# VectorE's 512-column mask, group norm and output operations of a scan as two halves of 256

## The chip, the cores and the metric

The kernel runs on one core of a Trainium2 chip. The metric is the device time of one execution in microseconds (us), the median of several runs. All times below are us unless marked ns. The engines are named as the profile names them: PE (TensorE, matrix products), DVE (VectorE), ACT (ScalarE), POOL (GpSimd) and SP (SyncE, whose queue starts most of the DMAs).

## The reference

The program is a decoder trunk of two layers on an input of 512 tokens by 2048 channels in float32. Layer 0 has a projection, attention, pooling and gates and is not touched. Layer 1 is an RWKV-7 time mixing with 32 heads of 64 channels. Six mixes of the input are projected to r, k, v, g, a decay w and a rate a; then a state of 64 x 64 per head runs over the tokens, and its output goes through a group norm, a bonus and a gate into the output projection:

```python
def step(state, inp):
    r_t, w_t, k_t, v_t, kk_t, a_t = inp
    sa = jnp.einsum('bhvk,bhk->bhv', state, -kk_t)
    state = (state * w_t[:, :, None, :]
             + sa[..., None] * (kk_t * a_t)[:, :, None, :]
             + v_t[..., None] * k_t[:, :, None, :])
    return state, jnp.einsum('bhvk,bhk->bhv', state, r_t)
...
o = wkv7_scan(r, decay, k, v, kk, a)
mean = jnp.mean(o, axis=-1, keepdims=True)
var = jnp.mean(jnp.square(o - mean), axis=-1, keepdims=True)
o = ((o - mean) * lax.rsqrt(var + GN_EPS)).reshape(B_, S, D) * gn_w + gn_b
bonus = jnp.sum(r * k * r_k, axis=-1, keepdims=True) * v
o = (o + bonus.reshape(B_, S, D)) * jax.nn.silu(g)
return o.astype(x.dtype) @ w_o
```

## The kernel before

Layer 0 and the projections k, r and g of layer 1 are large products in which every float32 operand is split into two parts and three products are summed (lines 137 to 147 and 506 to 508). The work around the change is the scan, `scan()`, which treats the 32 heads as 16 pairs of two heads, and the 512 tokens as 8 chunks of 64. A tile of one pair has 128 partitions (two heads of 64 channels, or 64 tokens of a chunk by two) and 512 or 1024 columns.

For each pair p there are seven generators; each `yield` ends a step:

- `vproj(p)` projects v for the pair: 48 products of 512 columns on PE (lines 145 to 147, tile vps), with the weights split by ACT (L137) and by POOL (L141, tile wlo).
- `gprod(p)` loads AR and BK, multiplies them chunk by chunk (L908, tile g in PSUM, two tiles of four chunks for each half b), and puts a triangular mask on them: L914 writes Z[h] from g[h] and mk, one operation of 512 columns for each half b and head h, four for a pair. Then BK is transposed (L920) and copied by ACT (L921).
- `lanes(p)` inverts the 16 x 16 diagonal blocks: POOL copies blocks of Z to nd (L950, four operations; two of them read Z[0], two Z[1]), DVE transposes (L955, tile lt) and adds (L957, tile la), then come 15 times a product (L962, tile pr) and a reduction (L963, tile uc) of growing size, each of which reads what the one before it wrote; ACT spreads the result (L969, tile e), DVE transposes (L971, tile tb), ACT writes DT (L973), DVE transposes it into U (L977). The tile uc is the same for all pairs.
- `levels(p)` extends the inverse to 64 x 64 with PE, ACT and DVE (L1000 to L1026).
- `vprep(p)` makes the bonus bv on POOL (L930), and the transposed v (L937, L940).
- `chain(p)` is the recurrence over the 8 chunks: PE's xo (L1044, L1047), copied to xs by DVE (L1051) and ACT (L1052); PE's sa (L1055), copied into RS by DVE (L1056); PE's s (L1062); DVE's new state M (L1071 or L1073) from s and ACT's m (L1066); PE's output (L1076), copied to O by ACT (L1079).
- `post(p)` is the group norm and the output of the pair: a sum over each head's 64 columns (L1091, tile gs), the subtraction of the mean in O (L1093), ACT's square (L1095), its sum (L1097), a reciprocal root in small operations (L209 to L220), the multiplication (L1100), four transposes on PE (L1104, tile ot), ACT's scale and shift (L1106, tile gm), the bonus and the gate (L1108, L1109), and a store or a split. Its DVE operations have 512 columns.

The scan is cut into periods of 12 slots, one pair each; in a slot, the chain of one pair and that of the next are advanced under a high priority (an offset of 400), and the steps of the other generators follow at planned times, given by constants such as LA = (8, 15) for the lanes of pair p + 3, GP = (0.5, 9) for its gprod and PO = (13.5, 20) for the post of pair p. PE's order is that of the program, by hand. On the other engines the framework sets the order: an instruction that is ready goes by its priority, which is its place in the program, or 400 places earlier for the chains.

Pools have few buffers: one uc, one nd2, one gs, two of the PSUM tiles g, bt, vt and ot together, three O, four Z of each head.

Of the kernel before, what the change touches and what calls it, by code (L numbers as in the profile page):

```python
# [12 lines left out]
ALU = mybir.AluOpType  # L13
AX = mybir.AxisListType
# [3 lines left out]
P = 128  # L18
# [16 lines left out]
class Kernel:  # L35
# [809 lines left out]
    def scan(self, ctx, xv, first, mp, ld, ar_d, bk_d, bc_d, g_d, m_d):  # L845
        nc, tc, i = self.nc, self.tc, self.i
# [47 lines left out]
        def gprod(p):  # L894

            s = sets[p]
            AR = s["AR"] = ld.tile([P, 8, 2, 64], F32, tag="AR", name="AR", bufs=4)
            nc.sync.dma_start(AR.rearrange("p a b c -> p (a b c)"), ar_d[p])
            BK = ld.tile([P, 8, P], F32, tag="BK", name="BK")
            nc.sync.dma_start(BK.rearrange("p a b -> p (a b)"), bk_d[p])  # L900
            yield

            Z = s["Z"] = [st.tile([P, 8, P], F32, tag=f"Z{h}", name=f"Z{h}", bufs=4) for h in range(2)]
            for b in range(2):
                g = [aux("g").rearrange("p (c n) -> p c n", c=4) for _ in range(2)]
                for c in range(4):
                    for h in range(2):
                        mm(g[h][:, c, :], BK[half[h], 4 * b + c, :],  # L908
                           AR[half[h], 4 * b + c].rearrange("p a b -> p (a b)"), start=True, stop=True)
                    if c == 1:  # L910
                        yield
                for h in range(2):
                    mk = self.mk[:, 64 * (p % 2):64 * (p % 2) + P]
                    nc.vector.tensor_mul(Z[h][:, 4 * b:4 * b + 4, :], g[h], mk.unsqueeze(1).to_broadcast([P, 4, P]))  # L914
                yield
            BT = s["BT"] = st.tile([P, 8, P], F32, tag="BT", name="BT")
            for b in range(2):
                g = aux("bt")
                for c in range(4):
                    nc.tensor.transpose(g[:, c * P:(c + 1) * P], BK[:, 4 * b + c, :], self.ident)  # L920
                nc.scalar.copy(BT[:, 4 * b:4 * b + 4, :], g.rearrange("p (c n) -> p c n", c=4))  # L921
                yield
# [160 lines left out]
        def post(p):  # L1083

            s = sets[p]
            gt = tp.tile([P, S], F32, tag="ldg", name="ldg")
            nc.sync.dma_start(gt, g_d[p])
            O = s["O"].rearrange("p t h n -> p (t h) n")
            sm = tp.tile([P, 8], F32, tag="gs", name="gs")
            bc = lambda t: t.unsqueeze(2).to_broadcast([P, 8, 64])  # L1090
            nc.vector.tensor_reduce(sm, O, AX.X, ALU.add)  # L1091
            yield
            nc.vector.scalar_tensor_tensor(O, bc(sm), -1.0 / 64, O, ALU.mult, ALU.add)  # L1093
            sq = tp.tile([P, 8, 64], F32, tag="pt", name="gsq")
            nc.scalar.activation(sq, O, AF.Square)  # L1095
            yield
            nc.vector.tensor_reduce(sm, sq, AX.X, ALU.add)  # L1097
            rs = self.rsqrt_eps(tp, sm, GN_EPS, 8, "gn", 1.0 / 64)
            yield
            nc.vector.tensor_mul(O, O, bc(rs))  # L1100
            yield
            g = aux("ot")
            for t in range(4):
                nc.tensor.transpose(g[:, t * P:(t + 1) * P], s["O"][:, t].rearrange("p h n -> p (h n)"), self.ident)  # L1104
            m = tp.tile([P, S], F32, tag="pt", name="gm")
            nc.scalar.activation(m, g, AF.Identity, scale=self.vec["gw"][:, p:p + 1], bias=self.vec["gb"][:, p:p + 1])  # L1106
            yield
            nc.vector.tensor_add(m, m, s["bv"])  # L1108
            nc.vector.scalar_tensor_tensor(m, m, 0.5, gt, ALU.mult, ALU.mult)  # L1109
            if p < 13:  # L1110
                nc.sync.dma_start(m_d[p], m)
            else:
                t = mixed[p] = mp.tile([P, 2, S], F32R, tag="mx", name="mixed")
                self.split(t[:, 0, :], t[:, 1, :], m)
            yield
# [67 lines left out]
        def plan_pair(base, q, skip=0):  # L1183

            gp = gprod(q)
            next(gp)
            plan(base, gp, 6, *GP)
            plan(base, hurry(lanes(q)) if q == 15 else lanes(q), 18, *LA)
            plan(base, hurry(levels(q)) if q == 15 else levels(q), 5, *LV)
            plan(base, vproj(q), 8, *VJ)  # L1190
            plan(base, vprep(q), 2, *VP)


        v, gp = vproj(0), gprod(0)
        next(gp)
        for q in range(2):
# [6 lines left out]
        for q in range(16):  # L1203
            next(la)
            if q % 2:
                next(v, None)
        g1, v = gprod(1), vproj(1)
        next(g1)
        run(la)
# [18 lines left out]
        for p in range(-1, 16):  # L1228
            at = 12 * (p + 1)
            if p + 3 < 16:  # L1230
                plan_pair(at, p + 3)
            if 0 <= p < 15:
                late = 1.2 if p in (13, 14) else 0
                plan(at, post(p), 6, PO[0] + late, PO[1] + late)
            if p == 13:
                plan(at, units(0, 1, 2), 3, *A13)
                plan(at, project(*both(0, 1, 2)), 6, *B13)
            if p == 14:
                plan(at, units(3, 4, 5, 6, 7), 5, *A14)
                plan(at, project(*both(3, 4, 5, 6, 7)), 10, *B14)  # L1240
                plan(at, project(*[(2, k) for k in range(3)]), 3, *Q14)
            if p == 15:
                plan(at, units(8, 9, 10, 11, 12, 13), 6, *A15)
                plan(at, project(*both(8, 9, 10, 11, 12, 13)), 12, *B15)
                plan(at, project(*[(2, k) for k in range(3, 10)]), 7, *Q15)
            B = chain(p + 1) if p < 15 else None
            slot(at, [c for c in (A, B) if c])
            A = B
        assert not todo
        g = post(15)  # L1250
        for _ in range(4):
            next(g)
# [87 lines left out]
```

## Time and profile before

| | us |
|---|---|
| median of 3 runs (lowest to highest) | 2084.72 (2082.19 to 2085.89) |
| the profiled execution | 2082.21 |
| its span, first to last instruction | 2080.4 |
| granted PE clock in it | 0.992 |
| 1390 to 1490, start of the scan: DVE busy | 77.69 of 100 |
| 1490 to 1580: DVE busy, PE busy | 78.90, 87.71 of 90 |
| 1580 to 1640: DVE busy, PE busy | 52.26, 57.44 of 60 |
| 1820 to 1880, end of the scan with the first output products: DVE, PE busy | 48.82, 52.98 of 60 |

The profile is that of one execution. An engine's busy time counts its computing instructions; matrix products are pipelined with modelled ends, so a busy PE is not PE at its peak. Rows of instructions name the line, the engine, the operation and the tiles as out<-in, with partitions x columns. A chain of waits follows the work that ended last back in time: at each step to what released it, or to the instruction before it on its engine. An instruction on DVE may start before the one ahead of it on DVE has ended, so the time from start to start can be less than a duration.

### The profile page before, as it was taken

Reading aid. Unit: us, or ns where it says so; the run is one execution under the profiler, and the core shown is the slowest. Engines: PE = TensorE matmul, PEld = TensorE weight load, DVE = VectorE, ACT = ScalarE, POOL = GpSimd, SP = SyncE. Lnnn points to the kernel's source line nnn. Section 1 sums busy time; section 2 is a strip of 40 time slices with the busy share of each in tenths; the row PEclk is TensorE's granted clock in tenths of the full one; section 3 lists DMA queues with packets and bytes.
Section 4 is the critical chain, followed back from the end, with each engine's and each line's share of the span. In section 5 each row is a group of like instructions: output and inputs, shape, how many; then the busy total and the mean of one; then the engine's idle time right before and its main releaser. Section 6 shows DMA issues by size and latency. Waiting matters only on the chain.

```text
span 2080.4 us, 33934 instructions
## 1 busy us (share of the span) xinstructions
PE 2016.8 (97%) x13091; PEld 1637.4 (79%) x13091; DVE 1282.0 (62%) x2572; ACT 961.5 (46%) x1687; POOL 282.7 (14%) x550
## 2 busy tenths in 40 slices
PE   8999999999999998999999999999999999989996
PEld 7888888888888897777878888886777777767786
DVE  5344345444433357666866676668788888886436
ACT  3345445323322138654745564454555555564221
POOL 0000000000000000234000000013444444410003
PEclk9999999999999999999999999999999999999998
DMA  5222222233333353465365556542223332232733
GB/s 195 92 81 81 81 81 66 86 97 100 98 111 112 115 169 126 138 180 178 118 213 190 181 171 218 198 166 67 91 76 106 109 108 89 95 118 92 245 105 111
DMA packets 214034, 262.99 MB, mean 126 GB/s; under 512 B 15769, under 2 KB 161777, under 8 KB 213105
## 3 DMA queue, kind: packets, MB, share of 16 engines
q1 hardware_dynamic: 213872, 260.83, 38.6%
q8 instruction: 103, 1.69, 0.3%
q14 instruction: 59, 0.48, 0.1%
HBM read 214.32 MB, written 46.47 MB: 125 GB/s over the span
## 4 chain that ended last, share of the span: by engine, by line
PE 77%; DVE 14%; ACT 3%; issue 2%; DMA 2%; POOL 1%; SPq 0%; DVEq 0%; ACTq 0%; POOLq 0%
PE ga L145 16%; PE ga L146 16%; PE ga L147 16%; PE gb L506 4%; PE gb L508 4%; PE gb L507 4%; DVE pr L962 2%; PE vps L145 2%; DVE uc L963 1%; DVE M L1071 1%; PE vps L146 1%; PE vps L147 1%; DVE RS L1056 1%; PE g L908 1%; PE y L506 1%
## 5 line engine op out<-in xcount | busy, mean ns | idle before, releaser
L141 DVE TENSOR_TENSOR wlo<-wraw,whi 128x1024 fp32r<-128x1024 f32 (+1 forms) x268 | 314.1, 1175 | 467.3 <-ACT whi L137 464.0
L137 ACT CAST whi<-wraw 128x1024 fp32r<-128x1024 f32 (+1 forms) x324 | 303.0, 938 | 545.2 <-PE ga L146 297.9
L145 PE MATMUL ga<-mx,whi 128*128 128x512 f32 x768 | 299.9, 391 | 3.2 <-ACT mx L137 3.2
L146 PE MATMUL ga<-mx,whi 128*128 128x512 f32 x768 | 300.4, 391 | 1.6 <-DVE mx L141 1.6
L145 PE MATMUL ga<-x,whi 128*128 128x512 f32 x768 | 300.5, 391 | 0.1
L147 PE MATMUL ga<-mx,wlo 128*128 128x512 f32 x768 | 300.3, 391 | 0.0
L147 PE MATMUL ga<-x,wlo 128*128 128x512 f32 x768 | 299.5, 390 | 0.5 <-DVE wlo L141 0.5
L146 PE MATMUL ga<-x,whi 128*128 128x512 f32 x768 | 299.2, 390 | 0.0
L508 PE MATMUL gb<-wlo,mixed 128*128 128x512 f32 (+1 forms) x576 | 197.4, 344 | 2.8 <-DVE wlo L141 2.8
L506 PE MATMUL gb<-whi,mixed 128*128 128x512 f32 (+1 forms) x576 | 198.0, 344 | 1.6 <-DVE s L457 1.6
L507 PE MATMUL gb<-whi,mixed 128*128 128x512 f32 (+1 forms) x576 | 197.5, 343 | 0.0
L145 PEld LDWEIGHTS ga<-mx,whi 128*128 128x128 f32 x768 | 144.8, 189 | 36.3 <-ACT mx L137 3.6
L146 PEld LDWEIGHTS ga<-mx,whi 128*128 128x128 f32 x768 | 144.9, 189 | 32.9 <-DVE mx L141 1.9
L147 PEld LDWEIGHTS ga<-mx,wlo 128*128 128x128 f32 x768 | 144.8, 189 | 30.6
L147 PEld LDWEIGHTS ga<-x,wlo 128*128 128x128 f32 x768 | 144.2, 188 | 31.2 <-DVE wlo L141 1.0
L145 PEld LDWEIGHTS ga<-x,whi 128*128 128x128 f32 x768 | 144.2, 188 | 29.6 <-ACT whi L137 0.4
L146 PEld LDWEIGHTS ga<-x,whi 128*128 128x128 f32 x768 | 144.3, 188 | 29.1
L141 POOL TENSOR_TENSOR wlo<-wraw,whi 128x128 fp32r<-128x128 f32 x224 | 100.3, 478 | 221.9 <-ACT whi L137 195.1
L508 PEld LDWEIGHTS gb<-wlo,mixed 128*128 128x128 f32 x576 | 109.4, 190 | 16.4 <-DVE wlo L141 3.7
L506 PEld LDWEIGHTS gb<-whi,mixed 128*128 128x128 f32 x576 | 109.5, 190 | 16.0 <-DVE s L457 3.3
L507 PEld LDWEIGHTS gb<-whi,mixed 128*128 128x128 f32 x576 | 109.6, 190 | 12.5
L145 PE MATMUL vps<-mx,whi 128*128 128x512 f32 x256 | 113.4, 443 | 0.8 <-ACT vT L891 0.8
(333 smaller groups left out, 3347.7 us busy)
## 6 DMA issues: line engine op xcount, KB each, us to landing
wraw<-in_ev_w_in SPq DMA_DIRECT2D x96, 512.0 KB, 3.6
wraw<-in_ev_w_out SPq DMA_DIRECT2D x32, 512.0 KB, 3.6
wraw<-in_od_w_k SPq DMA_DIRECT2D x32, 512.0 KB, 4.7
wraw<-in_od_w_r SPq DMA_DIRECT2D x32, 512.0 KB, 3.4
wraw<-in_od_w_g SPq DMA_DIRECT2D x32, 512.0 KB, 3.8
wraw<-in_od_w_v SPq DMA_DIRECT2D x64, 256.0 KB, 2.8
ar_d<-pAR SPq DMA_DIRECT2D x16, 512.0 KB, 2.6
bk_d<-pBK SPq DMA_DIRECT2D x16, 512.0 KB, 3.2
```

The lines of the kernel that those rows point to most:

```text
L137: self.nc.scalar.copy(hi, src)
L141: (eng or self.nc.vector).tensor_sub(lo[:, sl], src[:, sl], hi[:, sl].bitcast(F32))
L145: mm(ps, ah, bh, start=start, stop=False)
L146: mm(ps, ah, bl, start=False, stop=False)
L147: mm(ps, al, bh, start=False, stop=stop)
L506: mm(ps, ah, bh, start=start, stop=False)
L507: mm(ps, al, bh, start=False, stop=False)
L508: mm(ps, ah, bl, start=False, stop=stop)
L908: mm(g[h][:, c, :], BK[half[h], 4 * b + c, :], AR[half[h], 4 * b + c].rearrange("p a b -> p (a b)"), start=True, stop=True)
L962: nc.vector.tensor_mul(q, uc[:, :t, :t], la[:, t, :t].unsqueeze(1).to_broadcast([P, t, t]))
L963: nc.vector.tensor_reduce(uc[:, :t, t], q, AX.X, ALU.add)
L1056: nc.vector.tensor_copy(RS[a, c], sa[a])
```

## The change

In `scan()` the ten DVE operations of 512 columns in a pair's masks and post are issued as two operations of 256 columns each, with the same values:

```diff
@@ gprod
-                    nc.vector.tensor_mul(Z[h][:, 4 * b:4 * b + 4, :], g[h], mk.unsqueeze(1).to_broadcast([P, 4, P]))
+                    for c in (0, 2):
+                        nc.vector.tensor_mul(Z[h][:, 4 * b + c:4 * b + c + 2, :], g[h][:, c:c + 2], mk.unsqueeze(1).to_broadcast([P, 2, P]))
@@ post
-            bc = lambda t: t.unsqueeze(2).to_broadcast([P, 8, 64])
-            nc.vector.tensor_reduce(sm, O, AX.X, ALU.add)
-            yield
-            nc.vector.scalar_tensor_tensor(O, bc(sm), -1.0 / 64, O, ALU.mult, ALU.add)
+            for a in (0, 4):
+                nc.vector.tensor_reduce(sm[:, a:a + 4], O[:, a:a + 4], AX.X, ALU.add)
+            yield
+            bc = lambda t: t.unsqueeze(2).to_broadcast([P, 4, 64])
+            for a in (0, 4):
+                nc.vector.scalar_tensor_tensor(O[:, a:a + 4], bc(sm[:, a:a + 4]), -1.0 / 64, O[:, a:a + 4], ALU.mult, ALU.add)
             sq = tp.tile([P, 8, 64], F32, tag="pt", name="gsq")
             nc.scalar.activation(sq, O, AF.Square)
             yield
-            nc.vector.tensor_reduce(sm, sq, AX.X, ALU.add)
+            for a in (0, 4):
+                nc.vector.tensor_reduce(sm[:, a:a + 4], sq[:, a:a + 4], AX.X, ALU.add)
             rs = self.rsqrt_eps(tp, sm, GN_EPS, 8, "gn", 1.0 / 64)
             yield
-            nc.vector.tensor_mul(O, O, bc(rs))
+            for a in (0, 4):
+                nc.vector.tensor_mul(O[:, a:a + 4], O[:, a:a + 4], bc(rs[:, a:a + 4]))
...
-            nc.vector.tensor_add(m, m, s["bv"])
-            nc.vector.scalar_tensor_tensor(m, m, 0.5, gt, ALU.mult, ALU.mult)
+            for a in (slice(0, 256), slice(256, 512)):
+                nc.vector.tensor_add(m[:, a], m[:, a], s["bv"][:, a])
+                nc.vector.scalar_tensor_tensor(m[:, a], m[:, a], 0.5, gt[:, a], ALU.mult, ALU.mult)
```

The number of yields and their places, and everything on PE, ACT, POOL and the DMA queues, are as before.

## The prediction

> **What bounds the kernel now.** I read the page first, then a table of engine time by stage, then the chain of waits and the waits inside the scan, and last the single instructions of one period of the scan. Times are us unless marked ns. In a timeline row the columns are start, duration, engine, line, operation, output and input with their shapes, count, and in brackets the idle time before it with what ended that.
>
> From the page, the span, the busy time of each engine and the chain by engine:
>
> ```profile
> span 2080.4 us, 33934 instructions
> PE 2016.8 (97%) x13091; PEld 1637.4 (79%) x13091; DVE 1282.0 (62%) x2572; ACT 961.5 (46%) x1687; POOL 282.7 (14%) x550
> PE 77%; DVE 14%; ACT 3%; issue 2%; DMA 2%; POOL 1%; SPq 0%; DVEq 0%; ACTq 0%; POOLq 0%
> ```
>
> Over the whole span TensorE is the bound. The change lies in the scan alone, so its worth is read there. One row of the table by stage (busy us and instruction count per engine), then the chain of waits for the same 60 us by line, then what waited for whom from 1580 to 1820 (us, times, longest):
>
> ```profile
> 1640.00:1700.00 60.00, 57.85 (x736) 43.50 (x735) 52.28 (x170) 35.17 (x92) 26.82 (x53) 1.00 0.31 98
> by line: DVE pr L962 11.0%; DVE M L1071 9.3%; DVE uc L963 8.7%; issue 8.4%; DVE Z L914 6.8%; DVE RS L1056 6.3%; POOL nd L950 4.9%; DVE xs L1051 4.5%; DVE U L1013 2.6%; ACT DT L973 2.5%; DVE U L1026 2.5%; PE vps L145 2.2%; DVE gm L1108 2.1%;
> DVE lt L955 <- POOL nd L950: 13.1, 8, 1.6
> PE s L1062 <- DVE RS L1056: 6.8, 17, 0.7
> ```
>
> The reader is to see three things. VectorE is busy 52.28 of 60 us (87%) and nearly every line of the chain is its own; TensorE is busy too (57.85), but what it waits for is VectorE's RS. And VectorE's one long wait is for POOL's nd, 13.1 us in 8 periods, 1.6 each. So in the scan there is a loop: the lanes' inversion (pr and uc, 30 operations, each of which needs the one before it) runs on VectorE, then ScalarE and VectorE turn it, then the next pair's masks, POOL's nd, the transpose lt, and the next inversion. Here is one round of that loop on VectorE, first its start, then its late part and its end:
>
> ```profile
> 1644.71 0.71 DVE L955 STREAM_TRANSPOSE lt<-nd 128x512 f32<-128x512 f32 x1 [1.63 <-POOL nd L950]
> ...
> 1645.81 0.69 DVE L1108 TENSOR_TENSOR gm<-gm,bv 128x512 f32<-128x512 f32 x1
> 1646.42 0.42 DVE L957 TENSOR_TENSOR la<-lt 128x256 f32<-128x256 f32 x1
> 1646.75 0.69 DVE L1109 SCALAR_TENSOR_TENSOR gm<-gm,ldg 128x512 f32<-128x512 f32 x1
> 1647.47 0.61 DVE L1056 COPY RS<-sa 64x128 f32<-64x128 f32 x2
> ...
> 1656.91 0.24 DVE L963 TENSOR_REDUCE uc<-pr 128x9 f32<-128x81 f32 x1
> 1657.06 0.68 DVE L1091 TENSOR_REDUCE gs<-O 128x8 f32<-128x512 f32 x1
> 1657.65 0.26 DVE L962 TENSOR_TENSOR pr<-uc,la 128x100 f32<-128x100 f32 x1
> 1657.82 0.69 DVE L1093 SCALAR_TENSOR_TENSOR O<-gs,O 128x512 f32<-128x512 f32 x1
> 1658.54 0.48 DVE L1051 COPY xs<-xo 64x64 f32<-64x64 f32 x2
> 1658.94 0.24 DVE L963 TENSOR_REDUCE uc<-pr 128x10 f32<-128x100 f32 x1
> 1659.21 0.28 DVE L962 TENSOR_TENSOR pr<-uc,la 128x121 f32<-128x121 f32 x1
> 1659.42 0.68 DVE L1097 TENSOR_REDUCE gs<-gsq 128x8 f32<-128x512 f32 x1
> 1660.01 0.27 DVE L963 TENSOR_REDUCE uc<-pr 128x11 f32<-128x121 f32 x1
> 1660.32 0.31 DVE L962 TENSOR_TENSOR pr<-uc,la 128x144 f32<-128x144 f32 x1
> ...
> 1666.13 0.40 DVE L962 TENSOR_TENSOR pr<-uc,la 128x225 f32<-128x225 f32 x1
> 1666.44 0.68 DVE L1100 TENSOR_TENSOR O<-O,rsygn 128x512 f32<-128x512 f32 x1
> 1667.04 0.38 DVE L963 TENSOR_REDUCE uc<-pr 128x15 f32<-128x225 f32 x1
> 1668.09 0.61 DVE L1056 COPY RS<-sa 64x128 f32<-64x128 f32 x2 [0.67 <-PE sa L1055]
> ...
> 1669.24 0.65 DVE L914 TENSOR_TENSOR Z<-g,mk 128x512 f32<-128x512 f32 x1
> ...
> 1671.47 0.71 DVE L977 STREAM_TRANSPOSE U<-DT 128x512 f32<-128x512 f32 x1 [0.47 <-ACT DT L973]
> 1672.19 0.69 DVE L914 TENSOR_TENSOR Z<-g,mk 128x512 f32<-128x512 f32 x1
> 1674.51 0.71 DVE L955 STREAM_TRANSPOSE lt<-nd 128x512 f32<-128x512 f32 x1 [1.63 <-POOL nd L950]
> ```
>
> From lt at 1644.71 to the end of the last uc (1667.04 + 0.38 = 1667.42) VectorE shows no idle time: 22.7 us of a round of 29.80 (1674.51 − 1644.71). I call that stretch the sweep. In the 7.1 us behind it VectorE is idle three times, 0.67 + 0.47 + 1.63 = 2.8. Work moved from the sweep into those 2.8 us shortens the round; work added to the sweep lengthens it.
>
> **The change, priced.** Ten operations of 512 columns per pair (four masks, six in post) become twenty of 256. Nothing else is issued anew: no DMA, no PE, ScalarE or POOL instruction. Over 16 pairs that is 160 more VectorE instructions.
>
> The rows above have gm with 512 columns (0.69) and, between them, la with 256 columns (0.42). From start to start, where the next instruction doesn't need the result, gm took 0.61 (1645.81 to 1646.42) and la 0.33 (1646.42 to 1646.75). Two halves then take 0.66, which is 0.05 more than the whole. Where each half has to be waited out it is the durations that count, 2 × 0.42 − 0.69 = 0.15 more. A half of a reduction or of a scalar_tensor_tensor isn't in the trace. Its nearest rows are la, 0.42, and the reduction of 225 columns, 0.38; half of a 512 column row (0.34) is the floor, at which a split is free. I take 0.06 a split, next to the rows from start to start, since in the sweep the neighbours are mostly independent; both ends, 0 and 0.15, go to the range.
>
> What a half gives back. The inversion waits for itself: uc at 1658.94 (0.24) is followed by the pr that needs it after 0.27. With another operation between, uc at 1656.91 (also 0.24) gave way after 0.15. So a filler saves 0.12 of the step before it, and the order in the rows is a strict alternation: uc, gs, pr, O; pr, gs, uc. Never do two fillers follow each other while a pr or uc is ready. The inversion goes first, and the others take the gaps. A whole op in a gap delays the inversion by 0.60 − 0.12 = 0.48, a half by 0.33 − 0.12 = 0.21. The order of VectorE is not written by hand as PE's is; I expect the halves to keep this alternation, one in each of two gaps.
>
> The sum for a round:
> - Eight of the ten stand in the sweep (both gm, two gs, two O, two of the masks). Their splits cost 8 × 0.06 = +0.48.
> - The third mask, at 1669.24, stands ahead of the idle 0.47, which hides its 0.06; if that idle time went, it would cost the 0.06. The fourth, at 1672.19, is on the path behind U and is priced below.
> - Gaps that have no filler today and get one. Late in the sweep the rows show two, behind uc at 1658.94 (0.27 for 0.24) and behind uc at 1660.01 (0.31 for 0.27); I take three, and two early ones, to which the second halves of gm move (today both stand whole ahead of RS). 5 × 0.12 = −0.60. At the one end none is filled, 0; at the other each of the eight gains one, −0.96.
> - With more pieces than gaps ahead of the last uc, the latest piece of post, O at 1666.44, slips past it into the idle 0.67 or 0.47. The sweep loses 0.60 − 0.12 = −0.48. O isn't missed: the transposes that read it come in the next round.
> - Sum for the sweep: 0.48 − 0.60 − 0.48 = −0.60.
>
> What is late next. The end of the inversion frees ScalarE's e and DT, then U, Z at 1672.19, POOL's nd and lt. POOL's rows:
>
> ```profile
> 1643.15 1.52 POOL L950 TENSOR_TENSOR nd<-Z,md 32x256 f32<-32x256 f32 x2 [0.83 <-DVE Z L914]
> 1669.43 1.73 POOL L141 TENSOR_TENSOR wlo<-wraw,whi 128x128 fp32r<-128x128 f32 x4 [6.36 <-ACT whi L137]
> 1671.11 1.52 POOL L950 TENSOR_TENSOR nd<-Z,md 32x256 f32<-32x256 f32 x2
> ```
>
> In one kind of round POOL waits 0.83 for that Z, so up to 0.83 can be won. In the other, POOL starts its first two nd at 1671.11, behind its own wlo, and four of them end at 1671.11 + 4 × 0.76 = 1674.15; lt at 1674.51 can come only about 0.33 earlier. So of 0.60 I count 0.60 in one kind and 0.33 in the other, 0.46 in the mean, less 0.06 for the split of Z itself, which stands on this path: −0.40 a round. TensorE allows it: 60 − 57.85 = 2.15 of idle time in two rounds, about 1.1 each.
>
> Rounds: lt stands 16 times in the trace.
>
> ```profile
> L955 DVE STREAM_TRANSPOSE lt<-nd x16: 711/711/714, 1402.2 to 1821.3; 128x512 f32<-128x512 f32 x16
> ```
>
> The three or four at the start are the scan's filling, which PE and POOL set; about 12 are full rounds. 12 × −0.40 = −4.8. At the start, 12 masks at 0.06 are 0.7, of which the waits for POOL's nd hide about a half, +0.3 (all of it if they are hidden no longer); at the end stands post of pair 15, with six splits on the path, +0.4. Together −4.1, that is −0.2%.
>
> The profiled execution took 2082.21 for its span of 2080.4; with −4.1 it is 2078.1. The three runs have a median of 2084.72, 2.5 above it, so as a median I forecast 2080.6, rounded to 2080.5. A difference of about 0.2%, 4.2 us, is what a measurement can tell from no change, and the forecast lies on that edge.
>
> One rule speaks against the change. The Trainium skill, "VectorE: DVE Perf Modes", section "The DRAIN you can't avoid", says that after every VectorE operation the pipe is emptied and the next cannot issue before that; its rules for authors say to minimize the count of operations. The trace disagrees where neighbours are independent: la started 0.61 behind a gm of 0.69. The Trainium skill's section "Two Vector instructions with no wait between them" on that page allows an earlier start, and there the row agrees.
>
> **The rivals.**
> - *Each operation is paid to its end* (chance 0.04). If the halves must be waited out, for instance because a 64-row chain operation comes between them, a split is 0.15, and 160 of them, less the 12 at the start, are 148 × 0.15 = +22: 2107. For it: O at 1657.82, ahead of the 64-row xs, took its whole 0.69 and 0.03 more; against it: gm and la. The drain rule of the Trainium skill would give this case.
> - *The halves stay together* (0.24), the slower side. Place: the sweep. Both halves of an operation are issued in one step of post or gprod, so they may be taken one after the other; then no new gap is filled and nothing slips. Price: 10 × 0.06 a round × 12 = +7.2, and about +1 at the ends: 2084.7 + 8.2 = 2093. It decides against me as soon as fewer than half of the splits have a pr or uc between their halves. For it: today two fillers (O and xs) do stand together at 1657.82 and 1658.54; against it: xs is a chain operation with priority, and gs, O and gs each have one pr or uc behind them.
> - *All that leaves the sweep is won* (0.18). If POOL's wlo moves out of the way too, and the small reciprocal steps behind gs slip past the last uc as well, a round wins 0.60 plus a further 0.3: 12 × 0.9 = −11, 2074. Against it: that is nearly all of TensorE's idle 1.1 a round, and TensorE would become the bound.
> - *Another engine holds the round* (0.20). PE or POOL ends last and VectorE's gain becomes idle time; or gain and price cancel: −2 to +2, 2084.7. That the order doesn't change at all is not possible, since the count of instructions does.
>
> **Chances and range.** The forecast case has 0.34, with its own range of 2075 to 2084; six tenths of it lie below −0.2%. Faster by over 0.2%: 0.20 + 0.18 = 0.38. Slower: 0.24 + 0.04 = 0.28. Within: 0.14 + 0.20 = 0.34. The range goes from the third rival, 2072, to the halves together with a somewhat dearer split, 2094; the first rival is left out.
>
> **What would show it.** In the changed kernel, gs, O and gm stand as single halves with a pr or uc between; the stretch from lt to the last uc is about 22.1 instead of 22.7; the multiplication by rsygn stands behind the last uc; POOL's wait for Z shrinks from 0.83; rounds are 0.4 shorter in the mean. A pair of halves with start to start near 0.33 and nothing between is the second rival; 0.42 each is the first. Wrong altogether would be a sweep that is shorter while the rounds are not: then PE's idle time before s or q tells which engine holds them.

## The result and the profile after

With the change the kernel takes 2103.57 us (median of 4 runs, 2102.1 to 2104.82), beside 2083.45 (4 runs, 2081.92 to 2085.89) for the kernel before on the same chip: a ratio of 1.0101, 95% interval 1.0087 to 1.0115. It is slower by 20 us, or 1.0%; the forecast was 2080.5 in a range that ended at 2094.

The page of the changed kernel has the span, the busy time of each engine, and the chain by engine:

```profile
span 2103.1 us, 34090 instructions
PE 2021.9 (96%) x13091; PEld 1639.0 (78%) x13091; DVE 1292.7 (61%) x2732; ACT 961.4 (46%) x1687; POOL 284.4 (14%) x550
PE 76%; DVE 14%; ACT 3%; issue 3%; DMA 2%; POOL 1%; SPq 0%; DVEq 0%; ACTq 0%; POOLq 0%
```

The span is 22.7 longer, VectorE has its 160 instructions more and is busy 10.7 longer, and TensorE, with as many instructions as before, 5.1. That leaves 17.6 us more in which TensorE stands still. The row of lt says where they lie:

```profile
L956 DVE STREAM_TRANSPOSE lt<-nd x16: 671/711/714, 1401.4 to 1844.3; 128x512 f32<-128x512 f32 x16
```

Before, the 16 lt ran from 1402.2 to 1821.3, so 419.1; now they take 442.9. The whole loss (+23.8) lies between the first and the last lt. The stretch behind the last one is as long as before (2080.4 − 1821.3 = 259.1, and 2103.1 − 1844.3 = 258.8). For nine full rounds, from the 7th lt to the 16th, here is a row of the table by stretches (stretch and its length; then busy us and count of PE, PEld, DVE, ACT and POOL; the granted clock and the DMA columns), before and after:

```profile
1556.78:1821.27 264.49, 254.68 (x3243) 190.98 (x3243) 230.29 (x747) 152.72 (x396) 115.02 (x225) 1.00 0.32 100
```

```profile
1565.35:1844.35 279.00, 257.77 (x3245) 192.70 (x3244) 235.25 (x838) 154.04 (x396) 116.17 (x225) 0.99 0.30 95
```

A round grew from 29.39 to 31.00. VectorE is busy 4.96 longer with 91 instructions more, 0.055 for each. TensorE's idle time grew from 9.81 to 21.23, by 11.4 of the 14.5. The view of waits for the same nine rounds says what it waits for (us in all, times, longest), before and after, with VectorE's longest wait on top:

```profile
DVE lt L955 <- POOL nd L950: 14.7, 9, 1.6
PE s L1062 <- DVE RS L1056: 6.8, 17, 0.7
PE q L1000 <- ACT DT L973: 2.3, 4, 0.6
PE c L1000 <- ACT q L1021: 0.3, 1, 0.3
```

```profile
DVE lt L956 <- POOL nd L951: 25.7, 10, 2.6
PE g L908 <- DVE Z L915: 10.7, 9, 1.2
PE vps L145 <- ACT vT L891: 5.8, 8, 0.8
PE s L1063 <- DVE RS L1057: 2.6, 8, 0.5
PE c L1001 <- ACT q L1022: 1.6, 5, 0.3
...
POOL nd L951 <- DVE Z L915: 15.6, 9, 2.7
```

Among TensorE's waits one that the list of before doesn't have, 1.2 us in each round, has taken the first place: TensorE wants to write g and waits for the masks. VectorE's wait of lt for POOL's nd grew as well, from 1.6 to 2.6 us a time (the ten of the changed kernel take in the one ahead of the first lt). VectorE's rows of one changed round show what the masks do (start, duration, engine, line, operation, tiles, count, idle time before):

```profile
1657.83 0.71 DVE L956 STREAM_TRANSPOSE lt<-nd 128x512 f32<-128x512 f32 x1 [2.60 <-POOL nd L951]
...
1675.15 0.41 DVE L915 TENSOR_TENSOR Z<-g,mk 128x256 f32<-128x256 f32 x1
1675.49 0.57 DVE L1072 SCALAR_TENSOR_TENSOR M<-s,pcs,m 64x64 f32<-64x64 f32 x2
1676.10 0.58 DVE L1074 TENSOR_SCALAR M<-s,pcs 64x64 f32<-64x64 f32 x2
1676.71 0.33 DVE L964 TENSOR_REDUCE uc<-pr 128x13 f32<-128x169 f32 x1
1677.07 0.42 DVE L915 TENSOR_TENSOR Z<-g,mk 128x256 f32<-128x256 f32 x1
1677.41 0.35 DVE L963 TENSOR_TENSOR pr<-uc,la 128x196 f32<-128x196 f32 x1
1677.68 0.42 DVE L915 TENSOR_TENSOR Z<-g,mk 128x256 f32<-128x256 f32 x1
1678.01 0.35 DVE L964 TENSOR_REDUCE uc<-pr 128x14 f32<-128x196 f32 x1
1678.39 0.48 DVE L1052 COPY xs<-xo 64x64 f32<-64x64 f32 x2
1678.79 0.38 DVE L963 TENSOR_TENSOR pr<-uc,la 128x225 f32<-128x225 f32 x1
1679.09 0.41 DVE L915 TENSOR_TENSOR Z<-g,mk 128x256 f32<-128x256 f32 x1
1679.43 0.37 DVE L964 TENSOR_REDUCE uc<-pr 128x15 f32<-128x225 f32 x1
...
1680.32 0.76 DVE L1105 TENSOR_TENSOR O<-O,rsygn 128x256 f32<-128x256 f32 x2
...
1682.89 0.42 DVE L915 TENSOR_TENSOR Z<-g,mk 128x256 f32<-128x256 f32 x1
1683.23 1.19 DVE L1072 SCALAR_TENSOR_TENSOR M<-s,pcs,m 64x64 f32<-64x64 f32 x4
1684.45 0.71 DVE L978 STREAM_TRANSPOSE U<-DT 128x512 f32<-128x512 f32 x1
1685.18 1.09 DVE L915 TENSOR_TENSOR Z<-g,mk 128x256 f32<-128x256 f32 x3
1688.80 0.71 DVE L956 STREAM_TRANSPOSE lt<-nd 128x512 f32<-128x512 f32 x1 [2.53 <-POOL nd L951]
```

The four halves of b=0 stand one in each gap of the inversion, as forecast, and so the last of them ends only at 1679.50, 4.35 after the first began. In the kernel before the same two masks took 2.90:

```profile
1662.42 0.67 DVE L914 TENSOR_TENSOR Z<-g,mk 128x512 f32<-128x512 f32 x1
...
1664.63 0.69 DVE L914 TENSOR_TENSOR Z<-g,mk 128x512 f32<-128x512 f32 x1
```

The masks of b=1 are late too. Only one half of the third mask stands ahead of U; the other three halves stand behind it, from 1685.18. POOL needs both halves of the third mask for its first two nd, so all four now come behind U:

```profile
1685.68 3.08 POOL L951 TENSOR_TENSOR nd<-Z,md 32x256 f32<-32x256 f32 x4 [1.57 <-DVE Z L915]
```

In the kernel before, two of them started at 1671.11, ahead of the fourth mask (1672.19). From U to the next lt it is 4.35 us here and was 3.04.

TensorE's rows for g in that changed round, and then in the one before, from its timeline:

```profile
1677.95 0.48 PE L908 MATMUL g<-AR,BK 64*128 64x128 f32 x2
1679.56 0.71 PE L908 MATMUL g<-AR,BK 64*128 64x128 f32 x6 [1.12 <-DVE Z L915]
...
1684.15 0.50 PE L145 MATMUL vps<-mx,whi 128*128 128x512 f32 x1 [0.67 <-ACT vT L891]
```

```profile
1660.86 0.71 PE L908 MATMUL g<-AR,BK 64*128 64x128 f32 x8
...
1664.95 1.14 PE L908 MATMUL g<-AR,BK 64*128 64x128 f32 x8
```

The g of b=1 goes into the two PSUM tiles that hold the g of b=0. TensorE can write into the first at once and stops at the second until its mask has read it: 1679.50 is the end of the mask, 1679.56 the next product. Behind it in TensorE's order, which is by hand, stand the chains' products and vproj's, and all of them come later. In the kernel before, the same eight products show no idle time, but took 1.14 where their siblings took 0.71, and the second mask ended at 1665.32, in their midst. They were already at the point of waiting, which the prediction took no account of.

### The profile page after: what moved, and what is told of

Read it like the earlier page. It is cut to its first block, busy times and chain, and to the rows that moved or that the text cites. A ratio compares the mean times of both kernels' runs of the same rounds, so it can differ in the third digit from the quotient of the medians.

```text
span 2103.1 us, 34090 instructions
## 1 busy us (share of the span) xinstructions
PE 2021.9 (96%) x13091; PEld 1639.0 (78%) x13091; DVE 1292.7 (61%) x2732; ACT 961.4 (46%) x1687; POOL 284.4 (14%) x550
## 4 chain that ended last, share of the span: by engine, by line
PE 76%; DVE 14%; ACT 3%; issue 3%; DMA 2%; POOL 1%; SPq 0%; DVEq 0%; ACTq 0%; POOLq 0%
PE ga L147 15%; PE ga L146 15%; PE ga L145 15%; PE gb L508 4%; PE gb L506 4%; PE gb L507 4%; PE vps L145 2%; DVE pr L963 1%; PE vps L146 1%; PE vps L147 1%; DVE Z L915 1%; PE g L908 1%; DVE uc L964 1%; DVE M L1072 1%; POOL nd L951 1%
## 5 line engine op out<-in xcount | busy, mean ns | idle before, releaser
L146 PEld LDWEIGHTS ga<-x,whi 128*128 128x128 f32 x768 | 144.3, 188 | 29.4
L508 PEld LDWEIGHTS gb<-wlo,mixed 128*128 128x128 f32 x576 | 109.1, 190 | 16.9 <-DVE wlo L141 4.4
```

The costliest lines, as they stand in the source:

```text
L146: mm(ps, ah, bl, start=False, stop=False)
L508: mm(ps, ah, bl, start=False, stop=stop)
```

## The experiments

All compare with the kernel before on the same chip, and times given as over or under it are against its median there. The intervals are 2 to 4 us wide on each side, so smaller differences between two rows can't be told apart. The table gives the ratio with its interval, and of nine rounds (7th to 16th lt) their time, TensorE's busy and idle time, and its largest waits. In the expectations M and Q stand for the theory of the masks that TensorE waits for, Q its sharper form (g of b=1 behind the masks of b=0); L for the lanes' end as what holds the round; P for post and N for the count of instructions as the cause; H for VectorE's added work as such.

| kernel | ratio (95%) | nine rounds | PE busy, idle | PE's waits |
|---|---|---|---|---|
| before | 1 | 264.49 | 254.68, 9.81 | s 6.8, q 2.3 |
| changed | 1.0101 (1.0087–1.0115) | 279.00 | 257.77, 21.23 | g 10.7, vps 5.8 |
| masks alone halved | 1.0118 (1.0098–1.0137) | 280.49 | 259.44, 21.05 | g 11.2, sa 4.3 |
| post alone halved | 1.0014 (1.0004–1.0024) | 264.38 | 254.64, 9.74 | s 8.5, g 1.1 |
| b=0 masks alone | 1.0134 (1.0119–1.0149) | 283.48 | 260.90, 22.58 | g 11.3, s 6.2 |
| b=1 masks alone | 1.0054 (1.0039–1.0069) | 269.42 | 255.38, 14.04 | q 4.5, s 4.5 |
| changed, masks first | 1.0052 (1.0036–1.0068) | 270.37 | 256.96, 13.41 | s 7.5 |
| before, masks first | 1.0125 (1.0108–1.0142) | 283.18 | 258.93, 24.25 | sa 13.2 |
| mask halves glued | 1.0030 (1.0018–1.0041) | 269.89 | 259.95, 9.94 | s 5.6, q 4.1 |
| changed, mask halves glued | 1.0061 (1.0040–1.0081) | 272.28 | 257.85, 14.43 | s 6.5, g 5.8 |
| changed, g planned early | 1.0084 (1.0069–1.0099) | 275.87 | 261.14, 14.73 | q 6.2, s 4.6 |
| before, g planned early | 1.0022 (1.0012–1.0032) | 265.77 | 252.63, 13.14 | s 5.7, q 3.7 |
| changed, lanes' end first | 1.0170 (1.0154–1.0185) | 286.02 | 262.13, 23.89 | g 10.8, s 8.5 |
| before, lanes' end first | 1.0017 (1.0006–1.0027) | 264.46 | 255.50, 8.96 | s 7.3 |
| before, second mask late | 1.0010 (1.0000–1.0019) | 265.65 | 256.55, 9.10 | s 5.6, g 2.3 |
| all halves glued | 1.0044 (1.0028–1.0059) | 269.43 | 254.57, 14.86 | q 9.4, s 3.2 |
| two extra ahead of a mask | 1.0138 (1.0118–1.0158) | 280.87 | 259.56, 21.31 | g 16.9 |
| two extra behind it | 1.0118 (1.0101–1.0135) | 278.17 | 258.47, 19.70 | q 7.9, s 3.7 |

### Which part costs

The change with one of its two parts left out: the masks alone halved, and post alone halved.

> Only the four masks of a pair are done as halves; post is as before (64 of the 160 added instructions). Theory M (the masks carry the loss: their halves are taken apart, so that PE's product g waits for the last half of the first two masks and POOL's nd starts late): 16 to 22 us over before, PE's wait of g for Z about 1.1 us a round, VectorE's wait of lt for nd 2.5 a round instead of 1.6. Rival P (post carries it: four halves of gm stand ahead of la and RS): 0 to 3 over before. Rival N (the count of instructions carries it, 20 us over 160): 8 over before.

> Only post's six operations are done as halves; the masks are whole (96 of the 160 added instructions). Theory M: between 6 us faster and 2 slower than before; PE's g doesn't wait for Z. Rival P: 16 to 20 slower. Rival N: 12 slower.

The masks alone cost about as much as the whole change (+23.7 us beside +20.1, with intervals that overlap, and a little above what M expected), with the same wait for g. Post alone costs 2.5, and its nine rounds are those of before within 0.1 us. Yet its sweep, from lt to the end of the last uc, is 20.1 to 20.7 in these rounds where it had been 21.7 to 22.7. Here is its row of the stretches:

```profile
1560.83:1825.21 264.38, 254.64 (x3246) 190.34 (x3244) 232.61 (x801) 154.40 (x397) 113.81 (x225) 1.00 0.32 100
```

So 1.8 us taken out of a sweep in the mean (22.2 to 20.4) won nothing: the rest of the round, from the last uc to the next lt, grew from 7.2 to 9.0. Its 2.5 us lie in the early rounds, two of which are 31.2 and 31.7 instead of 29.0 and 29.5.

Then one half b of the masks at a time:

```diff
+                    if b == 0:   # the other kernel: b == 1
+                        for c in (0, 2):
+                            nc.vector.tensor_mul(Z[h][:, 4 * b + c:4 * b + c + 2, :], ...)
+                    else:
                         nc.vector.tensor_mul(Z[h][:, 4 * b:4 * b + 4, :], g[h], ...)
```

> Only the two masks of the first half (b = 0) are done as halves; the masks of b = 1 and post are whole. Theory Q (TensorE holds the round: a round is its 28.5 us of work and its waits; the halves of the b = 0 masks stand apart, and the product g of b = 1 needs their PSUM tiles): 10 to 18 us over before, PE's wait of g for Z about 1.2 a round. Rival L (the loop through nd and lt holds the round, the halves of the b = 1 masks stand apart behind U and POOL starts late): at most 4 over before.

> Only the two masks of the second half (b = 1) are done as halves. Theory Q: between 2 faster and 5 slower than before, since no product of the pair waits for these tiles; PE's g waits for Z less than 0.2 a round, even if lt waits for nd longer. Rival L: 10 to 18 over before, lt's wait for nd 2.5 a round.

The wait for g belongs to b=0 alone, as expected: 11.3 us against none. But the sizes were missed in both: b=0 alone cost 27.8 where 10 to 18 was expected, b=1 alone 10.5 where next to nothing was. b=1 halved makes waits of another kind (q for DT, vps for vT), and POOL waits 13.9 us for Z, nearly as long as in the changed kernel (15.6). The parts don't add up: 27.8 and 10.5, but 23.7 together and 20 with post.

### The order of the masks

If late masks are the cost, masks that go first should win it back. The edit is the same on the changed kernel and on the one before (the loop over h and all in it move into the block):

```diff
+                with tc.high_priority(offset=400):
-                for h in range(2):
+                    for h in range(2):
...
```

> The changed kernel, with the masks' halves under the same high priority as the chains (offset 400), so that the lanes' steps don't come between them; all 160 added instructions stay. Theory M: the loss goes, within 5 us of before on either side; no wait of g for Z over 0.3 us. Rival P: still 15 or more slower than before, as the halves of gm are not touched. Rival N: still 20 slower.

> The kernel before, whole operations, with the masks under the chains' high priority. Theory M: the masks' place is what counts, so 3 to 10 us faster than before; POOL's nd starts earlier after the masks. Rivals P and N: within 2 us of before, as nothing of theirs is touched.

On the changed kernel the wait for g is gone and half of the 20 us with it; 9.9 are left, where M expected no more than 5. Its sweep shrank to 18.7 to 19.0 us, and the round is still 30.0, longer than before, because 11.2 us now follow the sweep: again a shorter sweep alone wins nothing. On the kernel before, where a gain was expected, the result was 25.6 us slower. TensorE now waits for xs ahead of sa, 13.2 us in nine rounds. That expectation was plainly wrong; one wait was exchanged for a longer one, and why xs comes late there wasn't followed up.

Next, the halves kept together, so that each mask is split without the alternation, on the kernel before and on the changed one:

```diff
-                    nc.vector.tensor_mul(... whole, or the loop over two halves ...)
+                    first = nc.vector.tensor_mul(... half 1 ...)
+                    with tc.issue_after(first.ins), tc.high_priority(offset=400):
+                        nc.vector.tensor_mul(... half 2 ...)
```

> The masks as halves as in the change, post whole, and the second half of each mask issued right behind the first (an order on VectorE, with the chains' priority), so that no step of the lanes comes between. Theory Q: the loss is the place, not the count; between 2 faster and 5 slower than before, PE's g waits for Z less than 0.4 a round. Rival N (the count of instructions): 8 over before. Rival L: within 4 of before too.

> The changed kernel with all its 160 added instructions, the second half of each mask right behind the first. Theory Q: within 0 to 7 us of before (post's halves alone cost 2.5), 13 or more below the changed kernel; PE's idle time 1.0 to 1.4 a round instead of 2.4. Rival N: no change against the changed kernel, 20 over before.

With the four masks split but glued, the kernel costs 6 us over before, where the alternating halves cost 23.7, and there is no wait for g. So the wait came from the alternation and not from the split. The second halves also got the chains' priority, so the order isn't changed in this point alone; and 6, in an interval of 3.7 to 8.5, tells neither Q's 5 at most nor N's 8 from the other. With post halved as well, half of the wait is back (5.8 us in ten times) and the loss is 11.5, above the 7 expected at most. What makes the masks late there wasn't followed up.

Then all ten operations split and glued, which is the prediction's second rival built on purpose:

> All ten operations as halves, with the second half of each right behind the first: the count of the changed kernel and nearly the order of the kernel before. Theory Q: between 1 faster and 8 slower than before; in nine full rounds PE's idle time is 9 to 13 us (9.8 before, 21.2 changed), VectorE's busy time about 5 us more than before. Rival N: 20 slower, as in the change.

```profile
1560.16:1829.59 269.43, 254.57 (x3219) 191.64 (x3216) 239.47 (x838) 152.69 (x393) 112.81 (x225) 0.99 0.32 98
```

2092.16 us, against the 2093 that the rival gave: 10.7 over the kernel before on that chip, where the rival's sum was 8.2. Q fares worse: it allowed 8, and 9 to 13 us of idle time, and 14.9 were measured, with a wait for DT in the first place. Nearly the same instructions are issued as in the changed kernel (838 in nine rounds in both), and VectorE is even busier, 239.47 against 235.25; but the kernel is 9 to 12 us faster than the changed one. **The order in which the halves alternate with the inversion, which the prediction counted as a gain of 0.12 a piece, costs about half of the 20 us.**

### Other ways to take the wait away

The steps of gprod planned earlier, so that g and its masks come at another place of the round:

```diff
-            plan(base, gp, 6, *GP)
+            todo.extend((base + x, len(todo), gp) for x in (0.5, 1.2, 3.33, 4.75, 6.17, 7.58))
```

> The changed kernel with the second step of gprod, which holds the last products of b = 0 and their masks, planned at slot 1.2 instead of 1.9 of a round, and all else as planned; the same instructions. The masks of b = 0 then have 0.7 slots, about 1.8 us, more before the products of b = 1 need their PSUM tiles. Theory Q: PE's wait of g for Z falls from 1.2 a round to under 0.5, and the kernel is 6 to 18 us faster than the changed one. Rival L (the loop through U, nd and lt): no gain over 3 us, since the masks of b = 1 stay as they are. Rival N (the count): no gain.

> The kernel before with the same earlier step. Control: there PE's g doesn't wait for Z, so theory Q expects nothing to win: within 4 us of before. If it is 6 or more faster, the earlier step is good for another reason, and the run before it shows less of Q.

The wait for g is gone, but only 3 to 6 us of the 20 come back, where Q expected 6 to 18; the plan by itself costs the kernel before 4.7, a little more than the 4 allowed. The distance between the two kernels thus fell from 20 to about 11 to 13. The rest shows up as waits for DT (6.2) and as busier products, at a clock of 0.98.

Rival L: a priority for e, tb, DT and U, on the changed kernel and on the one before; and an order for the second mask of b=0 behind the lanes' latest uc, to make it late in the kernel before:

```diff
+            with tc.high_priority(offset=400):
+                e = tp.tile(...)
...
+            with tc.high_priority(offset=400):
+                nc.vector.transpose(U..., DT...)
@@ the other kernel, gprod
+                        if b == 0 and h == 1 and p > 2:
+                            order.enter_context(tc.issue_after(last_uc[0].ins))
                         nc.vector.tensor_mul(Z[h][:, 4 * b:4 * b + 4, :], g[h], ...)
```

> The changed kernel with the end of the lanes (e, tb, DT and U) under the chains' high priority, so that U and what stands behind it on VectorE come earlier. Rival L: most of the loss goes, within 6 us of before. Theory Q: the halves of the b = 0 masks still stand apart, so PE's g still waits for Z 0.8 or more a round and the kernel stays 10 to 22 over before.

> The kernel before with the end of the lanes under the chains' high priority. Theory Q: TensorE's idle time is 1.1 us a round and 0.3 of it is the wait of q for DT, so between 4 faster and 2 slower. Rival L: 5 to 10 faster.

> The kernel before, all operations whole, and only the second mask of b = 0 is issued behind the last uc of the lanes instead of ahead of it. Nothing is split. Theory Q: what costs is that the mask comes late for PE's next product g, whoever makes it late: PE's wait of g for Z between 0.5 and 1.8 a round, and 6 to 25 us over before. Rival N (the count) and rival H (only halves of 256 columns cost, by what they are): within 3 us of before.

L's gain didn't come: the changed kernel became 12 to 14 us slower still, 34 over before and above Q's 22 too, with the wait for g as it was; and the kernel before lost 4 where L expected a gain of 5 to 10. But VectorE's wait of lt for nd stayed at 2.6 us, so the edit didn't shorten the path that L names, and L isn't refuted by it. What speaks against L as the whole cause is b=0 alone, which cost 27.8 where L allowed 4. The third run came out 2.8 over before, within the 3 of N and H, but it tests little. The added order drew the lanes forward (sweeps of 20.4 to 21.1) more than it held the mask back (in one round 3.36 us from the start of the first mask to the end of the second, instead of 2.90), and TensorE waited no more than 0.4 at a time for it.

To make the masks of b=0 late without a split, two further products of 512 columns into a scratch tile were put either ahead of the second mask or behind it; otherwise the two kernels are the same:

```diff
+                        for op in (more, more, put):   # the other kernel: (put, more, more)
+                            with tc.issue_after(last.ins):
+                                last = op()
```

> The kernel before, nothing split, with two more VectorE operations of 512 columns a pair (products of the mask with itself into a scratch tile that nothing reads), ordered ahead of the second mask of b = 0. They make that mask late by 1.2 us or more, as the halves do in the change. Theory Q: PE's g waits for Z 0.8 to 1.6 a round and the kernel is 8 to 25 over before, and 6 or more over the next run, which has the same two operations. Rival H (it is VectorE's time that counts): the same as the next run within 3.

> The same two more operations, ordered behind the second mask of b = 0. Theory Q: PE's g doesn't wait for Z (under 0.3 a round); 0 to 9 over before, although VectorE has 1.2 us more work a round (16 us in all). Rival H: 12 to 18 over before, as is the run ahead.

The stretch and TensorE's waits of nine rounds, first with the work ahead of the mask, then with it behind:

```profile
1566.56:1847.43 280.87, 259.56 (x3248) 193.54 (x3246) 242.66 (x765) 155.53 (x397) 111.25 (x225) 0.98 0.30 94
PE g L909 <- DVE Z L915: 16.9, 9, 2.1
```

```profile
1561.29:1839.46 278.17, 258.47 (x3215) 193.20 (x3214) 244.73 (x765) 152.54 (x393) 115.86 (x225) 0.98 0.31 95
PE q L1010 <- ACT DT L983: 7.9, 3, 2.8
PE s L1072 <- DVE RS L1066: 3.7, 11, 0.5
```

A mask that comes late makes TensorE wait, 1.9 us in each round, without any halves; a mask in its old place doesn't. So it is shown that late masks stop TensorE. What the stop is worth is not: the two kernels are only 3.5 us apart, with intervals that overlap, where at least 6 was expected of Q. Both lost more than the 12 to 18 of H, and the second, 24.6 over before, far more than the 9 that Q allowed. With the extra work behind the mask TensorE waits about as long, for DT and others, and the round is longer by (278.17 − 264.49) / 9 = 1.52, which is the two products of 0.69 and a little more. **Work added to VectorE lengthens the round even when no mask is late.**

At last the wait taken away by a buffer: a third PSUM tile for g, bt, vt and ot, whose bank comes from sa and s1:

```diff
-        po = ctx.enter_context(tc.tile_pool(name="po", bufs=2, space=PSUM))
+        po = ctx.enter_context(tc.tile_pool(name="po", bufs=1, space=PSUM))
-        pa = ctx.enter_context(tc.tile_pool(name="pa", bufs=2, space=PSUM))
+        pa = ctx.enter_context(tc.tile_pool(name="pa", bufs=3, space=PSUM))
```

> The changed kernel with a third PSUM tile for g, bt, vt and ot together; the bank for it is taken from the tiles sa and s1 of the chains, which then share one tile in turn instead of two. Nothing else is edited. If what the change costs is TensorE waiting until the masks of b=0 have read the two tiles of g (10.7 us in nine rounds), that wait is gone, since g of b=1 finds a third tile for its first half and needs only the first mask's tile for its second, and TensorE's idle time in nine rounds falls from 21.2 to 10 to 14; the kernel with the change then stands 0 to 10 us over the kernel before with the same third tile, where it now stands 20 over. If the 20 us are VectorE's loop alone (longer for 160 more operations and another order), the distance between the two kernels stays at 15 to 22, and TensorE's idle time turns up ahead of s, q or sa. Sharing one tile between two chains can make TensorE wait ahead of sa and s in both kernels, so only the distance between the two counts.

> The kernel before with the third PSUM tile for g, bt, vt and ot, and one for sa and s1: the partner of the run above. TensorE doesn't wait for the masks in the kernel before, so the third tile has nothing to win there: 0 to 10 us slower than before, by the waits ahead of sa and s that the single tile brings.

The changed kernel took 2203.31 us (1.0588, 1.0569 to 1.0607), the one before 2212.62 (1.0626, 1.0604 to 1.0648). With one tile for sa and s1 TensorE waits so long for RS and M that a round is 36 to 42 us, where 0 to 10 us in all were expected of the kernel before, and nothing else can be seen in it. Neither kernel shows a wait for g from 1600 to 1900, and the changed one isn't the slower one there, but at another bound this doesn't settle how much of the 20 us the wait is worth.

## Why the prediction was wrong

**What bounds the kernel: half right.** The prediction had VectorE's loop as the bound, so that less work in the sweep means a shorter round. That is where it failed first. Post alone halved (sweep 1.8 shorter, rounds the same) and the changed kernel with its masks first (sweep 3.4 shorter, round 0.7 longer) show that a shorter sweep alone wins nothing, since what follows the sweep grew by as much or more. In the opposite direction added work does cost: 1.38 us added per round made it 1.52 longer, 0.42 of it by longer busy time of TensorE. TensorE is busy 28.3 of 29.4 in a round of before and has 1.1 to spare. It looks as if both engines were at the bound at once, so that an edit can lose by either and win by neither; no edit tried won by either, which agrees with that but doesn't prove it.

**The price of a split: right in the changed kernel.** 0.06 was taken, 0.055 measured. Where the halves stand together it is dearer: with all of them glued VectorE is busy 9.18 longer with 91 instructions more, 0.10 for each. The row of halves of the masks, from 1580 to 1820, and one of post:

```profile
L915 DVE TENSOR_TENSOR Z<-g,mk 128x256 f32<-128x256 f32 x64 | 25.5, 419 | 0.9
L1096 DVE SCALAR_TENSOR_TENSOR O<-gs,O 128x256 f32<-128x256 f32 x15 | 6.2, 413 | 0.0
```

They last 0.42 and 0.41; three masks that stand together take 1.09 (1685.18), so 0.34 from start to start. The total is near the 2107 of the first rival, each operation paid to its end, but not for its reason, which needs 0.15 a split. The rule in the Trainium skill, "VectorE: DVE Perf Modes", "The DRAIN you can't avoid", that the next operation can't issue before the pipe is empty, doesn't by itself agree with these 0.34. The same section of the Trainium skill adds that an operation which isn't held starts earlier, and that agrees. Its advice under "Rules for kernel authors" to keep the count of operations small came out right here by another way.

**The alternation and the sweep: right in kind.** Halves stand singly in the gaps. The sweep of the round shown is 21.97 (1657.83 to 1679.80), against a forecast of 22.1 instead of 22.7. But 22.7 is the longer of two kinds of round; over the nine, the mean went from 22.22 to 21.81, so 0.41 shorter where 0.60 was forecast. O's multiplication, which was to slip past the last uc, did so (L1105 from 1680.32) without any use to the round.

**What is late next: wrong in sign.** The prediction let the whole gain of the sweep, or most of it, through the path behind it (U, the masks of b=1, nd, lt), and added 0.06 there. Measured from the end of the last uc to the next lt, that path went from 7.17 to 9.19 in the mean of the nine rounds, 2.02 longer; with the 0.41 of the sweep that is the 1.61 by which a round grew. In the round shown 1.3 of it lie between U and lt, by the third mask, whose halves stand on both sides of U, and 0.6 ahead of U.

**The step that failed** is "What a half gives back", with "TensorE allows it" and the −0.40 of "What is late next" that rests on both. It took the masks for fillers that nobody waits for. The prediction had named who waits for Z on POOL, but not who waits for the masks' *reading* of g: TensorE, whose next g needs those PSUM tiles and whose order by hand lets nothing pass. A gap filled by half a mask instead of a whole one delays the second mask's end. This wait alone, 1.19 a round, is more than the 1.1 us that the prediction saw as TensorE's room. What was forecast as −0.40 a round came out as +1.61: TensorE's wait for the masks 1.19, other waits 0.08 in the balance (vps +0.64, c +0.14, s −0.47 and q −0.26 among them), and 0.34 of longer busy time. That is TensorE's side of the same 1.61 that VectorE's rows divide into −0.41 and +2.02. No run separates how much of it the stop ahead of g makes and how much the late nd: two extra operations ahead of a mask lost 28 us with hardly a wait of POOL for Z (1.2 us in nine rounds), and b=1 alone lost 10.5 without a wait for g.

**The ends: mis-sized.** For the start of the scan the prediction had +0.3; the six rounds up to the 7th lt lost (1565.35 − 1401.4) − (1556.78 − 1402.2) = 9.4, of which 3.4 are more wait for g (6.5 instead of 3.1 there). The end, forecast at +0.4, is −0.3.

**The forecast's own test held.** It said that a sweep that is shorter while the rounds are not would show it wrong altogether, and that TensorE's idle time would name the engine. It did, though ahead of g and not of s or q. POOL's wait for Z, forecast to shrink from 0.83, grew to up to 2.7.

**How the 20 us divide** is known only roughly. Gluing all halves, and planning g early, each leave 9 to 13 (the latter over the kernel before with the same plan); with the masks first it is 10. So about half goes with the order of the halves. That this half is the wait for g is likely but not shown: planning g early took that wait away and won back only 3 to 6, and moving the extra work behind the mask 3.5. The rest may be what twenty pieces in place of ten cost in a loop without slack; it is not traced piece by piece, and each order tried took away one wait and made another. That single kernels don't add up (b=0, b=1, post) agrees with this. No version tried is faster than the kernel before.

## What to carry to other kernels

Before a piece of work is called a filler, ask who waits for its inputs to come free, not only for its output: here an engine with an order by hand stood waiting for two PSUM tiles. Where one engine is busy 96% of a round and the steps of another fill it from end to end, shortening one stretch won nothing here and added work cost its full time. Measure the whole loop and not the stretch that the change shortens. Look for a group of products that takes longer than its siblings (1.14 for 0.71), which is a wait that the list of waits doesn't show. Splitting operations of an engine whose order the framework sets changes the order of everything around them, and that was worth more here than the 0.055 us a piece.

## What the runs showed of the hardware

The granted clock can fall to half behind one idle stretch of TensorE of 2 us. In the kernel with glued mask halves, TensorE's timeline has this row, and the table by stretches around it the following four:

```profile
1675.79 0.24 PE L1002 MATMUL q<-DT,N 64*64 64x32 f32 x1 [2.04 <-ACT DT L975]
```

```profile
1674.00:1676.00 2.00, 0.21 (x8) 0.21 (x8) 1.31 (x4) 1.46 (x3) 0.99 (x3) 1.00 0.39 115
1676.00:1677.00 1.00, 1.00 (x33) 0.96 (x30) 0.75 (x2) 0.04 (x1) 0.70 (x1) 1.00 0.00 0
1677.00:1680.50 3.50, 3.50 (x25) 3.01 (x25) 2.33 (x9) 1.78 (x5) 0.00 (x0) 0.51 0.02 5
1680.50:1708.00 27.50, 27.08 (x342) 19.80 (x342) 23.52 (x79) 15.91 (x41) 12.07 (x25) 1.00 0.35 107
```

The clock is 1.00 for another microsecond, then 0.51 for about 3.4, and then 1.00. Half speed for 3.4 us makes the products about 1.7 longer, which adds to the wait ahead of it. The glued masks have three such stretches in their nine rounds; with no more idle time than before (9.94 against 9.81), they lost 5.4, 5.3 of it by longer busy time, at a mean clock of 0.98 instead of 1.00, and 2% of 260 is 5.2. The kernel with b=0 alone shows the same behind three of its nine waits of 1.2 to 1.3. The changed kernel has it once, behind the wait of 1.24 that ended at 1833.70, so about 1.7 of its 3.1 us of longer busy time are the clock:

```profile
1835.25:1838.75 3.50, 3.50 (x26) 2.22 (x26) 1.65 (x5) 2.49 (x4) 1.71 (x4) 0.51 0.00 0
```

Not every such wait does it: with two extra operations ahead of a mask there are five of 2.08 to 2.09, and a slow stretch stands behind two of them. In the nine rounds of the kernel before, where no wait is over 0.7, there is none. The Trainium skill, "TensorE: Matmul & The Clock Gate", "HAM oscillation — how this bites in real kernels", gives as a rule no idle gaps above some 3.4 us. The length of the slow stretch agrees with the window it states; the limit doesn't, since 2.04 was enough here.
